# Stick-breaking weights transposed in halves of 64 rows side by side, next to the scores of heads 0 to 3

## The chip, the cores and the metric

The kernel runs on one core of one Trainium2 chip. The metric is the device time of one execution in microseconds (us), taken as the median of several runs. The profile comes from one further execution, recorded by the hardware profiler. Its engines are PE (TensorE matmuls), PEld (TensorE weight loads), DVE (VectorE), ACT (ScalarE), POOL (GpSimd) and SP (SyncE, which issues most of the DMAs).

## What is computed

Two layers over a sequence of 256 positions with 1024 channels, all in float32. Every layer normalizes x, projects it once into all branches, and adds W_out of three gated branches to x: eight heads of dilated attention (branch A), a gated linear recurrence after a short convolution (branch B) and four heads of stick-breaking attention (branch C). The change is in branch C. Cut to it, the reference is:

```python
def hybrid_layer(x, ...):
    hn = rms_norm(x, norm_gain)
    proj = jnp.einsum('bsd,de->bse', hn, w_in)
    a_q, a_k, a_v, a_g, b_x, b_g, c_q, c_k, c_v, c_g = jnp.split(proj, _in_split_points(), axis=-1)
    ...
    y = jnp.concatenate([y_a, y_b, y_c], axis=-1)
    return x + jnp.einsum('bse,ed->bsd', y, w_out)

def stick_breaking_attention(q, k, v):
    ...
        z = jnp.einsum('bhqd,bhkd->bhqk', q_blk, kf) * scale
        causal = key_pos[None, :] < t[:, None]
        log_keep = jnp.where(causal, jax.nn.log_sigmoid(-z), 0.0)
        tail = lax.cumsum(log_keep, axis=3, reverse=True)
        between = jnp.concatenate([tail[..., 1:], jnp.zeros_like(tail[..., :1])], axis=-1)
        weights = jnp.where(causal, jnp.exp(jax.nn.log_sigmoid(z) + between), 0.0)
        return jnp.einsum('bhqk,bhkd->bhqd', weights, vf)
```

## The kernel before, in words

Every projection is cut into chunks of 256 output channels (`CH_CQ`, `CH_CK`, `CH_AQ[0]`, `CH_AK[0]`, `CH_BX`, `CH_AQ[1]`, `CH_AK[1]`, `CH_CG`, `CH_BG` and so on, numbered in the order of their use). A chunk's weights come in two DMAs into staging tiles `st`, of which there are five (`WST`). ACT copies each half of a staging tile into `whi` in a rounded format that PE multiplies faster (line 109), DVE takes the remainder into `wlo` (line 110), and PE multiplies with both. A staging tile is free for the next DMA when both have read it, and `whi` and `wlo` have four buffers each. `weights()` and `ask()` say how far ahead of its use a chunk is requested.

`proj_b` multiplies one chunk in two halves, b = 0 and b = 1. A caller can hand it a function `mid`, whose PE work is put between the halves. PE's order is written by hand (`manual_schedule`); on the other engines a scheduler arranges the instructions of the program when the kernel is built, and each engine then runs its list from front to back.

PSUM has four banks of the pool `at` (tag "s"), three of the pool `pp` and one of `yp`. In layer 0 one `pp` bank holds both halves of a chunk. In layer 1 most chunks are `PAIRED`: each half has a `pp` bank of its own, which is emptied by ACT (`low`, line 335) and then by DVE (line 337).

For branch C, `sb_scores` makes the weights of its four heads, `sw[0..3]`, each a tile of 128 partitions and 384 columns, in 3 blocks of 128 columns. The product with the values needs them transposed. `turned` does that for four blocks at a time: four PE transposes of 128x128 fill one "s" bank, and one ACT copy (line 464) of 128x512 brings it into the tile `wv`. For the twelve blocks there are three such groups. The first stands between the two halves of `CH_BX` (as the `mid` of `conv`), the other two stand after its second half. Then comes the first half of `CH_AQ[1]`, then its `mid`, called `second`: it computes the scores of heads 0 to 3 of branch A (`dil_scores(0)`, PE line 497, four "s" banks: first heads 0 and 1, then heads 2 and 3) and their softmax on DVE (line 504) and ACT (line 83). Then the second half of `CH_AQ[1]`, `CH_AK[1]` and `CH_CG` follow. DVE also computes the convolution of branch B in this stretch (lines 544 and 546).

The transposed weights in `wv` are first read by `values` in `third`, in the `mid` of `CH_BG`, some 20 us later.

Of the kernel before, what the change touches and what calls it, by code (L numbers as in the profile page):

```python
# [12 lines left out]
AF = mybir.ActivationFunctionType  # L13
ALU = mybir.AluOpType

P = 128
# [5 lines left out]
HD = 64  # L22
# [26 lines left out]
def trunk_kernel(ctx: ExitStack, tc: tile.TileContext, x, first_x, first, wpack, prm_d, gatew, gains, consts, rope, out):  # L49
    nc = tc.nc  # L50
    act, dve, pe, gps = nc.scalar, nc.vector, nc.tensor, nc.gpsimd
# [6 lines left out]
    pp = ctx.enter_context(tc.tile_pool(name="pp", bufs=3, space=bass.MemoryType.PSUM))  # L58
    at = ctx.enter_context(tc.tile_pool(name="at", bufs=4, space=bass.MemoryType.PSUM))
    yp = ctx.enter_context(tc.tile_pool(name="yp", bufs=1, space=bass.MemoryType.PSUM))  # L60

    def bank(pool, tag):
        return pool.tile([P, 512], F32, name=tag, tag=tag)
# [6 lines left out]
    def dep(inst, on):  # L70
        tc.add_manual_dep(inst.ins, on.ins.name, nosync)
        return inst
# [3 lines left out]
    def table(name, behind=()):  # L76
        load = act.preload_act_table_set(name)  # L77
        for u in (*loaded["users"], *behind):
            dep(load, u)
        loaded["load"], loaded["users"] = load, []  # L80
# [6 lines left out]
    def v2(a, n=2):  # L87
        return a.rearrange("p (b t) -> p b t", b=n)
# [91 lines left out]
    ident = con[:, C_ID:C_ID + P]  # L180
# [116 lines left out]
    for l in range(L):  # L297
# [50 lines left out]
        def proj_to(dst, c, mid=None, sc=1.0):  # L348
            if l > 0 and c in PAIRED[l]:
                proj_b(c, mid, dst, sc)  # L350
            else:
                scaled(dst, proj_b(c, mid), sc)
# [80 lines left out]
        zs, sw = {}, {}  # L433
        halves = ((0, slice(0, 128)), (1, slice(128, 384)))

        def sb_scores():
# [9 lines left out]
            for h in range(NHC):  # L446
# [8 lines left out]
                                           diag[:, 255 - n:255][:, ::-1], 0.0, ALU.mult, ALU.add)  # L455
                dve.tensor_mul(w, bt, w)

        def turned(tiles, h0, gs, to):
            for g in gs:
                tp = bank(at, "s")  # L460
                for i in range(4):
                    h, j = divmod(4 * g + i, 3)
                    pe.transpose(tp[:, i * P:(i + 1) * P], tiles[h0 + h][:, j * P:(j + 1) * P], ident)  # L463
                act.activation(to[g], tp, AF.Copy)

        def turned_tile():
            wv = wk.tile([P, 1536], F32, name="wv", tag="wv", bufs=1)
            return [wv[:, i:i + 512] for i in range(0, 1536, 512)], by_head(wv[:, 0:1024], wv[:, 1024:1536])

        def by_head(a, b):  # L470
            first = [a[:, 0:384], a[:, 384:768], None, b[:, 128:512]]
            parts = [h if h is None else (h[:, 0:256], h[:, 256:384]) for h in first]
            parts[2] = a[:, 768:1024], b[:, 0:128]
            return parts
# [14 lines left out]
        def dil_scores(h0):  # L489
            sps = {}  # L490
            for p in (h0, h0 + 2):
                for h in (p, p + 1):
                    sps[h] = bank(at, "s")
                for t, cs in halves:
                    for h in (p, p + 1):
                        hr, hb, _ = head(h - h0)
                        pe.matmul(sps[h][:, cs], qT[h0][hr, hb, t * P:(t + 1) * P], kT[h0][hr, hb, 0:(t + 1) * P],  # L497
                                  start=True, stop=True)
            shifted = {}
            for h in range(h0, h0 + 4):  # L500
                xs = scr(384)
                mn = wk.tile([P, 2], F32, name="mn", tag="mn", bufs=4)
                for t, cs in halves:
                    dve.tensor_tensor_reduce(xs[:, cs], sps[h][:, cs], nmask[:, cs], -0.125, 3e38,  # L504
                                             ALU.add, ALU.min, mn[:, t:t + 1])
                shifted[h] = xs, mn
            return shifted

        def dil_softmax(shifted):
            for h, (xs, mn) in shifted.items():  # L510
                pr = wk.tile([P, 384], F32, name="pr", tag="pr", bufs=4)
                den = wk.tile([P, 2], F32, name="den", tag="den", bufs=4)
                for t, cs in halves:
                    tab(pr[:, cs], xs[:, cs], AF.Exp, bias=mn[:, t:t + 1], scale=-1.0, accum_out=den[:, t:t + 1])
                dve.reciprocal(den, den)
                for t, cs in halves:
                    dve.tensor_scalar(pr[:, cs], pr[:, cs], den[:, t:t + 1], None, ALU.mult)
                prob[h] = pr

        def dil_transposes(h0):  # L520
            if h0 == 0:
                a = sb.tile([P, 1024], F32, name="pa", tag="yh1")
                b = sb.tile([P, 512], F32, name="pb", tag="yl1")
                to, heads = (a[:, 0:512], a[:, 512:1024], b), by_head(a, b)
            else:
                to, heads = turned_tile()
            turned(prob, h0, range(3), to)
            return heads

# [10 lines left out]
        def conv(mid):  # L540
            dve.memset(bxp[:, :, 0:3], 0.0)
            proj_to(bxp[:, :, 3:259], CH_BX, mid)
            for b in range(2):
                dve.tensor_scalar(xc[:, b, :], bxp[:, b, 3:259], prm[:, b, 3:4], prm[:, b, 4:5], ALU.mult, ALU.add)
                for j in (2, 1, 0):
                    dve.scalar_tensor_tensor(xc[:, b, :], bxp[:, b, j:j + 256], prm[:, b, j:j + 1], xc[:, b, :],
                                             ALU.mult, ALU.add)
            for j in range(2):
                gps.dma_start(out=xs[j * HD:(j + 1) * HD], in_=xc[(1 - j) * HD:(2 - j) * HD])
# [47 lines left out]
        rotate(proj_b(CH_AQ[0], sb_scores), qT, 0, "q0")  # L597
        rotate(proj_b(CH_AK[0]), kT, 0, "k0")
        sw_t, sw_heads = turned_tile()
        conv(lambda: turned(sw, 0, (0,), sw_t))  # L600
        turned(sw, 0, (1, 2), sw_t)
        y_c = {}

        def second():
            table(LN_EXP)
            dil_softmax(dil_scores(0))

        rotate(proj_b(CH_AQ[1], second), qT, 4, "q1")
        rotate(proj_b(CH_AK[1]), kT, 4, "k1")
        table(SIGM)  # L610
        cg_ps = proj_b(CH_CG)
        pts = dil_transposes(0)
        silu(cg, cg_ps)

# [27 lines left out]
        for n2 in range(2):  # L642
            w = weights(l, CH_O + n2)
            for t in range(NT):
                o_ps[t, n2] = bank(at, "s") if (t, n2) == (0, 0) else bank(pp, "pp")
                out_mm(o_ps[t, n2], w, t, 0, range(4), True, False)
                if (t, n2) == (0, 0):
                    y_c["p"] = dil_transposes(4)
                if (t, n2) == (0, 1):
                    emit_y(values(va, y_c["p"], 4), ag[:, 2:4, :], 6, 2)  # L650
# [125 lines left out]
```

## Time and profile before

| | us |
|---|---|
| median of 3 runs | 249.78 (249.46 to 250.14) |
| the profiled execution's own time | 248.82 |
| its span, first to last instruction | 246.7 |
| PE busy (matmuls) | 239.0 |
| DVE busy | 196.5 |
| ACT busy | 167.2 |
| POOL busy | 12.1 |
| mean granted TensorE clock | 0.996 |

The profiled execution's time is 2.1 us over its span, which is work around the program's own instructions, and 0.96 us under the median of the runs. An instruction row gives the start in us from the start of the span, the length, the engine, the line of the kernel, what it writes and reads, and the number of instructions merged in the row; in brackets stands the idle time before it and what ended it. A row of the chain of waits gives start, length and the work on the path that ended last. A busy PE row is modelled at its end, since matmuls overlap; differences between starts are the safer numbers.

### The profile page before, as it was taken

Reading aid. Unit: us, or ns where it says so; the run is one execution under the profiler, and the core shown is the slowest. Engines: PE = TensorE matmul, PEld = TensorE weight load, DVE = VectorE, ACT = ScalarE, POOL = GpSimd, SP = SyncE. Lnnn points to the kernel's source line nnn. Section 1 sums busy time; section 2 is a strip of 40 time slices with the busy share of each in tenths; the row PEclk is TensorE's granted clock in tenths of the full one; section 3 lists DMA queues with packets and bytes.
Section 4 is the critical chain, followed back from the end, with each engine's and each line's share of the span. In section 5 each row is a group of like instructions: output and inputs, shape, how many; then the busy total and the mean of one; then the engine's idle time right before and its main releaser. Section 6 shows DMA issues by size and latency. Waiting matters only on the chain.

```text
span 246.7 us, 4531 instructions
## 1 busy us (share of the span) xinstructions
PE 239.0 (97%) x1657; PEld 212.1 (86%) x1657; DVE 196.5 (80%) x442; ACT 167.2 (68%) x360; POOL 12.1 (5%) x45
## 2 busy tenths in 40 slices
PE   8999999999999999999999999999999999999990
PEld 4889999999998899878889988889889889987870
DVE  3885699999999799985792766999999987985253
ACT  3778989735947499964662885865498649992142
POOL 0037000001000000000100000000010000000000
PEclk9999999999999999999999999999999999999998
DMA  6989889268447741277157486605553672000022
GB/s 201 404 292 403 342 288 333 96 215 268 134 157 255 258 117 56 85 240 284 74 189 232 142 268 243 200 7 165 161 157 119 197 262 98 0 0 3 0 85 85
DMA packets 13173, 43.89 MB, mean 178 GB/s; under 512 B 1632, under 2 KB 2144, under 8 KB 13152
## 3 DMA queue, kind: packets, MB, share of 16 engines
q1 hardware_dynamic: 12384, 42.30, 51.1%
q10 hardware_dynamic: 576, 0.79, 0.9%
q0 software_dynamic: 192, 0.52, 0.7%
q8 instruction: 13, 0.21, 0.4%
q14 instruction: 8, 0.07, 0.1%
HBM read 42.03 MB, written 1.05 MB: 175 GB/s over the span
## 4 chain that ended last, share of the span: by engine, by line
PE 94%; DMA 2%; DVE 1%; ACT 1%; SPq 0%; issue 0%; ACTq 0%
PE pp L211 51%; PE pp L332 11%; PE s L211 9%; PE pp L329 5%; PE s L169 4%; PE s L463 3%; PE s L497 2%; PE y L427 2%; DMA st<-first 2%; PE pp L169 2%; PE s L443 1%; PE pp L427 1%; PE s L557 1%; PE s L259 1%; DVE xres L668 0%; ACT scr L242 0%
## 5 line engine op out<-in xcount | busy, mean ns | idle before, releaser
L110 DVE TENSOR_TENSOR wlo<-st,whi 128x512 fp32r<-128x512 f32 x132 | 84.1, 683 | 12.8 <-ACT whi L109 12.5
L109 ACT ACTIVATE whi<-st 128x512 fp32r<-128x512 f32 x132 | 73.9, 629 | 28.0 <-PE pp L211 11.8
L211 PE MATMUL pp<-xx,whi 128*128 128x256 f32 x480 | 63.3, 285 | 0.0
L211 PEld LDWEIGHTS pp<-xx,whi 128*128 128x128 f32 x480 | 59.7, 191 | 1.4 <-issue 1.3
L211 PE MATMUL pp<-xx,wlo 128*128 128x256 f32 x240 | 33.7, 283 | 0.0
L211 PEld LDWEIGHTS pp<-xx,wlo 128*128 128x128 f32 x240 | 30.9, 192 | 0.0
L332 PE MATMUL pp<-xx,whi 128*128 128x512 f32 x112 | 29.3, 396 | 0.0
L332 PEld LDWEIGHTS pp<-xx,whi 128*128 128x128 f32 x112 | 20.1, 189 | 4.1 <-ACT scr L83 0.3
L77 ACT ACT_TABLE_LOAD x13 | 16.7, 1283 | 1.9 <-PEq L769 1.7
L83 ACT ACTIVATE pr<-scr,mn 128x128 f32<-128x128 f32 (+1 forms) x32 | 14.1, 442 | 5.2 <-DVE mn L504 5.2
L329 PEld LDWEIGHTS pp<-xx,wlo 128*128 128x128 f32 x112 | 15.3, 190 | 1.1
L329 PE MATMUL pp<-xx,wlo 128*128 128x256 f32 x112 | 15.6, 282 | 0.0
L211 PE MATMUL pp<-whi,yh 128*128 128x512 f32 x48 | 14.5, 403 | 0.0
L211 PE MATMUL pp<-wlo,yh 128*128 128x512 f32 x48 | 14.0, 393 | 0.0
L211 PE MATMUL pp<-whi,yl 128*128 128x512 f32 x48 | 14.0, 393 | 0.0
L335 ACT ACTIVATE low<-pp 128x256 f32<-128x256 f32 x14 | 5.3, 382 | 9.1 <-PE pp L332 6.8
L211 PEld LDWEIGHTS pp<-wlo,yh 128*128 128x128 f32 x48 | 9.0, 188 | 2.1
L211 PEld LDWEIGHTS pp<-whi,yl 128*128 128x128 f32 x48 | 9.0, 188 | 2.0
L211 PEld LDWEIGHTS pp<-whi,yh 128*128 128x128 f32 x48 | 8.6, 188 | 2.0 <-issue 0.3
L169 PE MATMUL s<-whi,xx 128*128 128x512 f32 (+1 forms) x36 | 10.2, 404 | 0.1
L415 ACT ACTIVATE yh<-scr 128x512 fp32r<-128x512 f32 x8 | 5.0, 631 | 7.7 <-DVE scr L413 7.6
L504 DVE CUSTOM_DVE_ANT_0 scr<-s,con 128x128 f32<-128x128 f32 (+1 forms) x32 | 9.2, 351 | 0.0
(165 smaller groups left out, 355.2 us busy)
## 6 DMA issues: line engine op xcount, KB each, us to landing
st<-w_pack SPq DMA_DIRECT2D x66, 512.0 KB, 5.4
st<-first SPq DMA_DIRECT2D x7, 512.0 KB, 6.2
xres<-x_in SPq DMA_DIRECT2D x2, 512.0 KB, 8.1
gw_t<-gate_w SPq DMA_DIRECT2D x2, 256.0 KB, 6.9
gn<-gains SPq DMA_DIRECT2D x1, 512.0 KB, 6.7
xs<-xc POOLq DMA_DIRECT2D x4, 128.0 KB, 3.7
gf<-gains SPq DMA_DIRECT2D x1, 512.0 KB, 6.8
out<-scr SPq DMA_DIRECT2D x2, 256.0 KB, 2.1
```

The costliest lines, as they stand in the source:

```text
L77: load = act.preload_act_table_set(name)
L83: i = dep(act.activation(*a, **k), loaded["load"])
L109: split[l, c] = act.activation(hi[:, ws], st[:, ss], AF.Copy)
L110: dve.tensor_sub(lo[:, ws], st[:, ss], hi[:, ws].bitcast(F32))
L169: pe.matmul(ps[t][:, c0 - base:c1 - base], a[:, k, t * P:(t + 1) * P], b[:, c0:c1], start=k == 0 and i == 0 and c0 == base, stop=k == NK - ...
L211: pe.matmul(ps, a(k), b(k), start=first and i == 0, stop=last and i == len(seq) - 1)
L329: pe.matmul(ps[:, 0:S], lo[:, k, cs], xh[:, k, :], start=False, stop=False, skip_group_check=True)
L332: pe.matmul(ps, hi[:, k, cs], xx[:, k].rearrange("p h t -> p (h t)"), start=i == 0, stop=i == len(seq) - 1, skip_group_check=True)
L335: act.activation(low, ps[:, S:2 * S], AF.Copy, scale=sc)
L427: pe.matmul(y[hr, p * 128 + o:p * 128 + 256], vt[:, s0, hs], wts[i][s0], start=s0 == 0, stop=s0 == 1)
L463: pe.transpose(tp[:, i * P:(i + 1) * P], tiles[h0 + h][:, j * P:(j + 1) * P], ident)
L504: dve.tensor_tensor_reduce(xs[:, cs], sps[h][:, cs], nmask[:, cs], -0.125, 3e38, ALU.add, ALU.min, mn[:, t:t + 1])
```

## The change

The four weight tiles are transposed by a new function `turned_rows`. It takes each block of 128x128 as two halves of 64 rows (r = 0 and r = 64). Each half is a PE transpose of its own, with 64 rows of the block as the stationary operand and a 64x64 piece of the identity as the moving one, and it writes 64 columns of the output. The two halves of a block go to two different PSUM banks, and in the program they follow each other, so that rows 0 to 63 and rows 64 to 127 of the array are used in turn. Blocks 0 to 7 fill two "s" banks; blocks 8 to 11 fill half of each of two `pp` banks. ACT then empties the four banks with four copies (line 467 of the changed kernel), two of 8 runs of 64 columns and two of 4 runs, into the interleaved places of `wv`.

The place changes too. Nothing stands between or behind the halves of `CH_BX` any more. All 24 transposes stand at the beginning of `second`, directly ahead of the scores of heads 0 to 3. Since `CH_BX` has no `mid` now, its `weights()` call requests one chunk more at its start instead of after its first half.

```diff
+        def turned_rows(tiles, to):
+            for b0, b1, pool, tag in ((0, 8, at, "s"), (8, 12, pp, "pp")):
+                tps = [bank(pool, tag) for _ in range(2)]
+                for b in range(b0, b1):
+                    h, j = divmod(b, 3)
+                    for tp, r in zip(tps, (0, HD)):
+                        pe.transpose(tp[:, (b - b0) * HD:(b - b0 + 1) * HD],
+                                     tiles[h][r:r + HD, j * P:(j + 1) * P], ident[r:r + HD, r:r + HD])
+                for tp, r in zip(tps, (0, HD)):
+                    act.activation(to[:, b0:b1, r:r + HD], v2(tp[:, 0:(b1 - b0) * HD], b1 - b0), AF.Copy)
...
-        conv(lambda: turned(sw, 0, (0,), sw_t))
-        turned(sw, 0, (1, 2), sw_t)
+        conv(None)
         y_c = {}
 
         def second():
+            turned_rows(sw, v2(sw_t, 12))
             table(LN_EXP)
             dil_softmax(dil_scores(0))
```

How this moves instructions is seen on three engines. The first place is ACT's list in layer 0, from the table load after the sigmoids of branch C to the first exponential of the softmax; `whi<-st` is the splitting of weights, `wv<-s` the copy out of a transpose bank.

```order
 L77 ACT_TABLE_LOAD
-L109 ACTIVATE whi<-st 128x512 x4
-L464 ACTIVATE wv<-s 128x512
-L109 ACTIVATE whi<-st 128x512 x2
-L464 ACTIVATE wv<-s 128x512 x2
-L109 ACTIVATE whi<-st 128x512 x2
+L109 ACTIVATE whi<-st 128x512 x8
+L467 ACTIVATE wv<-s 128x8x64 x2
+L467 ACTIVATE wv<-pp 128x4x64 x2
 L83 ACTIVATE pr,den<-scr,mn 128x128
```

The same eight splits stand there. Before, the copies stood among them and two splits were left behind the last copy; now all four copies stand behind all eight splits.

The second place is PE's list in layer 1, with buffer numbers and with what each row waits for. Before, from the scores of heads 2 and 3 (`s_2221`, `s_2222`) over the second half of `CH_AQ[1]` (`pp_2285`) to the first half of `CH_AK[1]` (`pp_2326`):

```order
L497 MATMUL s_2221<-k0_2103,q0_2042 128x128 [waits Activation_49]
L497 MATMUL s_2222<-k0_2103,q0_2042 128x128 [waits Activation_49]
L497 MATMUL s_2221<-k0_2103,q0_2042 128x256
L497 MATMUL s_2222<-k0_2103,q0_2042 128x256
L332 MATMUL pp_2285<-xx_1583,whi_2048 128x512 x7
L329 MATMUL pp_2285<-xx_1583,wlo_2049 128x256 x8
L332 MATMUL pp_2285<-xx_1583,whi_2048 128x512
L332 MATMUL pp_2326<-xx_1583,whi_2137 128x512 [waits DVE_49]
```

The same stretch now, where the second half of `CH_AQ[1]` is `pp_2313` and the first half of `CH_AK[1]` is `pp_2354`:

```order
L508 MATMUL s_2249<-k0_2117,q0_2056 128x128 [waits Activation_49]
L508 MATMUL s_2250<-k0_2117,q0_2056 128x128 [waits Activation_49]
L508 MATMUL s_2249<-k0_2117,q0_2056 128x256
L508 MATMUL s_2250<-k0_2117,q0_2056 128x256
L332 MATMUL pp_2313<-xx_1597,whi_2062 128x512 [waits DVE_49]
L332 MATMUL pp_2313<-xx_1597,whi_2062 128x512 x6
L329 MATMUL pp_2313<-xx_1597,wlo_2063 128x256 x8
L332 MATMUL pp_2313<-xx_1597,whi_2062 128x512
L332 MATMUL pp_2354<-xx_1597,whi_2125 128x512 [waits Activation_49]
```

The scores of heads 2 and 3 wait for ACT in both, but now for the copies of the two "s" banks that were filled directly ahead. The second half of `CH_AQ[1]` waits for DVE now: of the three `pp` banks two hold transposes, so it takes the bank of its own first half, which DVE has to empty. The first half of `CH_AK[1]` takes a bank that ACT empties.

The third place is DVE's list in layer 1, from the emptying of the second half of `CH_BX` (`bxp<-pp,low`) to that of the first half of `CH_AQ[1]` (`scr<-pp,low`); `xc` is the convolution, `wlo<-st,whi` the splitting of weights. Before:

```order
L337 TENSOR_TENSOR bxp<-pp,low 128x256
L546 SCALAR_TENSOR_TENSOR xc<-bxp,prm_t,xc 128x256
L544 TENSOR_SCALAR xc<-bxp,prm_t 128x256
L110 TENSOR_TENSOR wlo<-st,whi 128x512
L546 SCALAR_TENSOR_TENSOR xc<-bxp,prm_t,xc 128x256
L110 TENSOR_TENSOR wlo<-st,whi 128x512
L546 SCALAR_TENSOR_TENSOR xc<-bxp,prm_t,xc 128x256
L110 TENSOR_TENSOR wlo<-st,whi 128x512
L546 SCALAR_TENSOR_TENSOR xc<-bxp,prm_t,xc 128x256
L337 TENSOR_TENSOR scr<-pp,low 128x256
```

Now:

```order
L337 TENSOR_TENSOR bxp<-pp,low 128x256
L558 SCALAR_TENSOR_TENSOR xc<-bxp,prm_t,xc 128x256
L556 TENSOR_SCALAR xc<-bxp,prm_t 128x256
L558 SCALAR_TENSOR_TENSOR xc<-bxp,prm_t,xc 128x256 x2
L110 TENSOR_TENSOR wlo<-st,whi 128x512
L558 SCALAR_TENSOR_TENSOR xc<-bxp,prm_t,xc 128x256
L337 TENSOR_TENSOR scr<-pp,low 128x256
```

Between the two rows stand two splits fewer than before, and the first of them has moved ahead of one step of the convolution; that step and the two splits now follow behind the last row.

More of the change, by code (lines that the diff above doesn't have):

```diff
@@ L467, in turned_tile @@
             wv = wk.tile([P, 1536], F32, name="wv", tag="wv", bufs=1)
-            return [wv[:, i:i + 512] for i in range(0, 1536, 512)], by_head(wv[:, 0:1024], wv[:, 1024:1536])
+            return wv, by_head(wv[:, 0:1024], wv[:, 1024:1536])
         def by_head(a, b):
@@ L525, in dil_transposes @@
             else:
-                to, heads = turned_tile()
+                wv, heads = turned_tile()
+                to = [wv[:, i:i + 512] for i in range(0, 1536, 512)]
             turned(prob, h0, range(3), to)
```

## The prediction

> **What bounds the kernel now.** I read the page first: the busy times and the chain that ended last.
>
> ```profile
> PE 239.0 (97%) x1657; PEld 212.1 (86%) x1657; DVE 196.5 (80%) x442; ACT 167.2 (68%) x360; POOL 12.1 (5%) x45
> ...
> PE 94%; DMA 2%; DVE 1%; ACT 1%; SPq 0%; issue 0%; ACTq 0%
> ```
>
> Then the busy times by window, for the stretch between PE's first projection matmul and its last, and for the stretch around the change in layer 1 (columns: the window, then for PE, PEld and DVE the busy us and instructions).
>
> ```profile
> 8.20:240.30 232.10, 232.10 (x1628) 207.44 (x1628) 190.21 (x424) 162.55 (x350) 11.69 (x36) 1.00 0.53 178
> 168.33:176.76 8.43, 8.43 (x61) 7.12 (x59) 8.43 (x20) 4.80 (x10) 0.00 (x0) 1.00 0.58 185
> ```
>
> PE is busy in 232.10 of 232.10 us. So the kernel is PE's list, run without a gap. Two things follow. PE work that is saved counts in full, and so does any wait that PE gets, since nothing later absorbs it. In layer 1 DVE too is busy in 8.43 of 8.43 us: whoever waits there for DVE waits for its list.
>
> The chain of waits gives the stretch of layer 0 (from the end of the first half of `CH_BX` to the end of the scores of heads 0 to 3) and that of layer 1.
>
> ```profile
> 50.66 0.44 PE s L463 x4
> 51.09 2.88 PE pp L211 x24
> 53.98 0.88 PE s L463 x8
> 54.85 2.86 PE pp L211 x24
> 57.72 1.51 PE s L497 x16
> 59.23 14.59 PE pp L211 x120
> ...
> 75.14 2.87 PE pp L211 x24
> ...
> 168.33 0.44 PE s L463 x4
> 168.77 1.62 PE pp L332 x7
> 170.39 0.95 PE pp L329 x8
> 171.34 0.23 PE pp L332
> 171.57 0.88 PE s L463 x8
> ...
> 175.25 1.51 PE s L497 x16
> 176.76 1.82 PE pp L332 x7
> ```
>
> Twelve transposes cost 0.44 + 0.88 = 1.32 us per layer, 0.11 each. A half of a chunk costs 2.87 us in layer 0 and 1.62 + 0.95 + 0.23 = 2.80 in layer 1. The scores next to them cost 1.51. The row at 75.14 is the first half of `CH_BG`.
>
> **The transposes themselves.** The trace has no transpose of 64 rows. The nearest row is the scores (L497), which also run 64 rows at a time in two halves of the array.
>
> ```profile
> L463 PE MATMUL s<-con,sw 128*128 128x128 f32 x24 | 3.3, 272 | 0.0
> L497 PE MATMUL s<-k,q 64*128 64x256 f32 x32 | 4.8, 377 | 0.0
> L497 PE MATMUL s<-k,q 64*128 64x128 f32 x32 | 3.5, 297 | 0.0
> ```
>
> One group of scores is 16 issues, half of them of 256 columns and half of 128. If they run in pairs and time goes with columns, 1.51 us is 4 pairs of one length and 4 of twice that, so a pair of 128 columns takes at most 1.51 / 12 = 0.126 us, and a pair of 64 columns 0.063. Twelve pairs then cost 0.76 us. Other ends: each pair at the price of a whole transpose today, 12 x 0.11 = 1.32; no pairing at all, 24 x 0.11 = 2.64. I take 0.76, since the scores are the nearest row. That saves 0.56 us per layer, if nothing waits.
>
> **The copies in layer 0.** What waits is the second half of the scores. Heads 2 and 3 take the two "s" banks that the transposes have just filled, so ACT must copy both out first. In ACT's list these copies now stand behind all eight splits. Here is ACT around that place, before.
>
> ```profile
> 53.34 1.15 ACT L109 ACTIVATE whi<-st 128x512 fp32r<-128x512 f32 x2 [3.91 <-DMA st<-w_pack]
> 54.40 0.58 ACT L464 ACTIVATE wv<-s 128x512 f32<-128x512 f32 x1
> 54.88 1.16 ACT L109 ACTIVATE whi<-st 128x512 fp32r<-128x512 f32 x2
> 55.94 1.06 ACT L464 ACTIVATE wv<-s 128x512 f32<-128x512 f32 x2
> 58.04 1.15 ACT L109 ACTIVATE whi<-st 128x512 fp32r<-128x512 f32 x2 [1.04 <-DMA st<-w_pack]
> ```
>
> The last pair of splits starts at 58.04, after 1.04 us of waiting for its DMA. It belongs to the second half of `CH_BG`, which PE needs only at 75.14. Before, the copies were done by 57.0, ahead of it. Now they stand behind it. That this transfer does not come earlier is read from the queue's own waits and from the staging tile's landings, of six transfers between 48 and 60 us and of sixteen between 30 and 75:
>
> ```profile
> SPq L106 <- DVE wlo L110: 147.3, 54, 10.8
> ...
> DMA to landing us min/median/max: 4.5/5.1/5.8
> ...
> DMA to landing us min/median/max: 3.6/5.2/6.4
> ```
>
> The issues wait for DVE to free a staging tile, and DVE's list up to there is unchanged. The shortest of the six, 4.5 us, puts the issue at about 53.5 (58.04 - 4.5), and a slower landing makes the splits later.
>
> So in layer 0: the halves of `CH_BX` and `CH_AQ[1]` follow each other without transposes between, 50.66 + 2.88 + 2.86 = 56.40. Transposes to 57.16, the scores of heads 0 and 1 (half of 1.51) to 57.92. ACT begins the first copy about 0.1 before the splits end, as its rows overlap (54.88 + 1.16 against 55.94): 59.09. Two copies, 1.06, end at 60.15. With 0.1 for the hand-over (an estimate, over the 0.03 and 0.04 that ACT's rows of layer 1 below take behind PE) PE goes on at 60.25 and ends the scores at 61.00, against 59.23. **Layer 0: +1.77 us**, with a wait of PE of about 2.3. Behind the waiting matmul stands all of PE's work, since its list is in order. The saving of 0.56 is inside that wait: at 1.32 for the transposes the result is the same, and at 2.64 too (56.40 + 2.64 + 0.76 = 59.80, still before 60.25).
>
> Were ACT free at that moment, the copies alone would set the pace: blocks 0 to 7 are there at 56.40 + 8 x 0.063 = 56.91, two copies end at 58.0, heads 2 and 3 run from 58.1 to 58.86, a gain of 0.37. The loss above comes from the late turn of the copies and not from their length.
>
> [...]
>
> **The bank in layer 1.** ACT keeps up with PE here. Its rows before: a copy directly behind the transposes (PE's row ends at 168.33 + 0.44 = 168.77), `low` of the first half of `CH_AQ[1]` directly behind that half (it ends at 175.25), and an idle stretch ahead of the softmax.
>
> ```profile
> 168.80 0.60 ACT L464 ACTIVATE wv<-s 128x512 f32<-128x512 f32 x1
> ...
> 175.29 0.38 ACT L335 ACTIVATE low<-pp 128x256 f32<-128x256 f32 x1 [0.24 <-PE pp L332]
> 179.12 0.40 ACT L83 ACTIVATE pr<-scr,mn 128x128 f32<-128x128 f32 x1 [3.45 <-DVE mn L504]
> ```
>
> The second half of `CH_AQ[1]`, though, needs the bank of its first half, and DVE empties that. DVE's rows before:
>
> ```profile
> 173.41 0.68 DVE L110 TENSOR_TENSOR wlo<-st,whi 128x512 fp32r<-128x512 f32 x1
> 174.02 0.48 DVE L546 SCALAR_TENSOR_TENSOR xc<-bxp,prm_t,xc 128x256 f32<-128x256 f32 x1
> 174.41 0.42 DVE L337 TENSOR_TENSOR bxp<-pp,low 128x256 f32<-128x256 f32 x1
> 174.75 0.48 DVE L546 SCALAR_TENSOR_TENSOR xc<-bxp,prm_t,xc 128x256 f32<-128x256 f32 x1
> 175.14 0.41 DVE L544 TENSOR_SCALAR xc<-bxp,prm_t 128x256 f32<-128x256 f32 x1
> 175.47 0.69 DVE L110 TENSOR_TENSOR wlo<-st,whi 128x512 fp32r<-128x512 f32 x1
> 176.07 0.48 DVE L546 SCALAR_TENSOR_TENSOR xc<-bxp,prm_t,xc 128x256 f32<-128x256 f32 x1
> ...
> 178.46 0.41 DVE L337 TENSOR_TENSOR scr<-pp,low 128x256 f32<-128x256 f32 x1
> ```
>
> From start to start a split takes 0.60, L546 0.39, L337 0.34, L544 0.33. In the new order, from 173.41: split to 174.02, `bxp` (L337) to 174.36, then L546 174.75, L544 175.08, two L546 175.86, split 176.46, L546 176.85, and L337 ends 0.42 later, at 177.27. With 0.1 for the hand-over PE goes on at 177.37.
>
> PE gets there at 168.33 + 2.80 + 2.80 = 173.93, transposes to 174.69, heads 0 and 1 to 175.45. The copies: `low` of `CH_AQ[1]` is done at 173.93 + 0.04 + 0.38 = 174.35, the last of blocks 0 to 7 at 173.93 + 0.51 = 174.44; two copies end at 175.53, and heads 2 and 3 run from 175.63 to 176.39. Then the wait for DVE, 0.98 us, to 177.37, against 176.76. **Layer 1: +0.61 us.** Unpaired transposes (2.64) would put the end of the scores at 173.93 + 2.64 + 1.51 = 178.08, +1.32. If that bank were free, it would be 176.39, -0.37.
>
> The rest I put at nothing: ACT has one copy more (0.3 us by half of L464's 0.58), in a place where it then waits for the softmax; the earlier request for weights leaves SP's order of transfers as it was; the first read of `wv` is 20 us away. PE resumes in a full stream behind each wait, and DVE, ACT and the DMAs then lead it by more than before.
>
> **Sum:** 1.77 + 0.61 = +2.38 us. Against the profiled execution's own 248.82 (span 246.7 and 2.1 around it) that is 251.2. The median of the runs is 0.96 above that execution; the prediction is for the median, 249.78 + 2.38 = 252.2.
>
> **The rivals.**
> - *The copies come in time: faster.* If the transfer for `CH_BG` were there 2.4 us earlier, or the copies got their turn ahead of the splits, and the bank were free, both layers would gain 0.37: 249.0. With no copy in the way at all it would be 2 x 0.56 = 1.12: 248.7. It decides at 57.92: the second copy must be done by then, so the splits by about 56.9 and the landing by 55.7, 2.2 us after the issue. The shortest of the landings above, 4.5, speaks against it, and so does ACT's order. Chance 0.08.
> - *No change.* Waits as in the first rival, but each pair takes the 0.11 of today's transpose. Then the copies start 0.35 later in each layer and the two gains shrink to about nothing: 249.8. Chance 0.08. [...]
> - *Only layer 0 waits.* The bank is free in time: +1.77 - 0.37 = 1.40, 251.2. For it speaks that DVE's list could run a little earlier behind the wait of layer 0; against it that DVE is full in the stretch. Chance 0.14.
> - *The change doesn't do what it says.* The halves run one after the other: 1.77 + 1.32 = 3.09, 252.9. Against it speaks that 16 score issues fit in 1.51 us. Chance 0.15.
> - My forecast, both waits with paired halves: 0.55.
>
> **How the numbers follow.** 0.3% is 0.75 us, about what a measurement of this kernel can tell from no change. Three cases end above it, 0.55 + 0.14 + 0.15 = 0.84 for slower, 0.08 each for the same and faster. For the range: with only layer 0 waiting and its transfer landing after 3.6 us, the shortest of the sixteen, instead of 4.5, it is 249.78 + 1.40 - 0.9 = 250.3; with the slowest of the six, 5.8, my forecast becomes 249.78 + 2.38 + 1.3 = 253.5. So 250.3 to 253.5, which leaves out the first two rivals, 0.16.
>
> **What would show it.** In the profile after: PE with a gap of 2 us or so at about 58 us, ended by ACT's copy (L467), and ACT's copies directly behind a split that waited for its DMA; a second gap of 0.5 to 1 us in layer 1 at the second half of `CH_AQ[1]`, ended by DVE's L337; the 24 transposes in 0.7 to 0.8 us. I am wrong if PE has no gap there, if the copies start before 58 us, or if the transposes take over 1.4.

## The result, and the profile after

The changed kernel takes 251.88 us (median of 6 runs, 251.44 to 256.57), the kernel before 249.88 (6 runs): ratio 1.0079, 95% interval 1.0061 to 1.0097, slower by about 2.0 us (0.79% of 249.88). Forecast were 252.2 and a range of 250.3 to 253.5. The run of 256.57 us, at a mean granted clock of 0.978, is left out of the ratio; there is no trace of it.

The profiled execution took 252.11 us with a span of 250.1. The busy times and the chain that ended last, now:

```profile
PE 239.2 (96%) x1681; PEld 211.0 (84%) x1681; DVE 196.5 (79%) x442; ACT 167.5 (67%) x362; POOL 11.4 (5%) x45
...
PE 77%; DVE 12%; DMA 4%; ACT 4%; issue 2%; SPq 0%; DVEq 0%; ACTq 0%
```

The busy times have hardly moved; the chain has. Before, it was PE for 94%; now a sixth of it runs over DVE and ACT, so PE's list is no longer without gaps. In layer 0 it leaves PE at 39.82 and runs over DVE's list, up to the split that frees the staging tile for one transfer (L110, 54.34 to 54.96). How it gets back to PE from there is in the chain itself (start, length, what):

```profile
54.98 3.91 DMA st<-w_pack
58.88 0.02 issue
58.91 1.15 ACT whi L109 x2
60.06 0.49 ACT wv L467
60.55 0.04 issue
60.59 0.48 PE s L508 x2
61.08 0.00 issue
61.08 0.92 PE s L508 x4
62.00 4.01 PE pp L211 x32
```

Read from the top: a transfer of weights, the two splits that wait for it, the first copy of the transposes, and only then PE's scores of heads 2 and 3. The timeline of the same place, PE and ACT, says how long PE stood:

```profile
57.82 0.71 PE L464 MATMUL s<-con,sw 64*128 64x64 f32 x16
58.37 0.41 PE L464 MATMUL pp<-con,sw 64*128 64x64 f32 x8
58.62 0.88 PE L508 MATMUL s<-k,q 64*128 64x128 f32 x8
60.59 1.41 PE L508 MATMUL s<-k,q 64*128 64x128 f32 x8 [1.10 <-ACT wv L467]
...
58.91 1.15 ACT L109 ACTIVATE whi<-st 128x512 fp32r<-128x512 f32 x2 [1.59 <-DMA st<-w_pack]
59.96 1.06 ACT L467 ACTIVATE wv<-s 128x512 f32<-128x512 f32 x2
```

The 24 transposes start at 57.82 and the scores behind them at 58.62: 0.80 us, where the twelve whole ones took 1.32, so the pairs do overlap. PE then idles for 1.10 us until the first copy is done, and the rows behind 60.59 stretch to 1.41 because head 3 waits once more, for the second copy (it ends at 59.96 + 1.06 = 61.02; PE's next step in the chain starts at 61.08).

Layer 1, PE and DVE:

```profile
176.57 0.71 PE L464 MATMUL s<-con,sw 64*128 64x64 f32 x16
177.12 0.56 PE L464 MATMUL pp<-con,sw 64*128 64x64 f32 x8
177.47 1.91 PE L508 MATMUL s<-k,q 64*128 64x128 f32 x16
179.59 0.41 DVE L337 TENSOR_TENSOR scr<-pp,low 128x256 f32<-128x256 f32 x1
180.06 1.89 PE L332 MATMUL pp<-xx,whi 128*128 128x512 f32 x7 [0.69 <-DVE scr L337]
```

The second gap, 0.69 us, ends with DVE's L337, as forecast, at the second half of `CH_AQ[1]`.

To compare kernels I take one stretch per layer out of each chain or timeline: from the start of the stick-breaking scores (L443) to the end of the scores of heads 0 to 3. Before it is 37.43 to 59.23 and 155.44 to 176.76, now 38.91 to 62.00 and 158.18 to 180.06. So layer 0 goes from 21.80 to 23.09, **+1.29**, and layer 1 from 21.32 to 21.88, **+0.56**: +1.85 together, which the measured 2.0 (0.0061 to 0.0097 of 249.88 is 1.5 to 2.4) holds. The spans differ by more, 3.4 us, but most of the rest stands ahead of the change: the stretch of layer 0 already begins 1.48 later. The first loads of weights, before and after:

```profile
1.64 4.93 DMA st<-first
```

```profile
1.65 6.08 DMA st<-first
```

They took 1.15 us longer in this execution. The kernels below start their stretch anywhere between 37.9 and 38.9 us, and the medians average over that.

### The profile page after: what moved, and what is told of

The parts are those of the page before. It is cut to its first block, busy times and chain, and to the rows that moved or that the text cites. A ratio compares the mean times of both kernels' runs of the same rounds, so it can differ in the third digit from the quotient of the medians.

```text
span 250.1 us, 4578 instructions
## 1 busy us (share of the span) xinstructions
PE 239.2 (96%) x1681; PEld 211.0 (84%) x1681; DVE 196.5 (79%) x442; ACT 167.5 (67%) x362; POOL 11.4 (5%) x45
## 4 chain that ended last, share of the span: by engine, by line
PE 77%; DVE 12%; DMA 4%; ACT 4%; issue 2%; SPq 0%; DVEq 0%; ACTq 0%
PE pp L211 44%; PE s L211 9%; PE pp L332 6%; PE s L169 4%; PE pp L329 3%; DVE wlo L110 3%; DMA st<-first 2%; PE y L427 2%; PE s L474 2%; PE pp L169 2%; PE s L508 2%; DMA st<-w_pack 2%; DVE sw L454 1%; ACT scr L83 1%; DVE scr L492 1%
## 5 line engine op out<-in xcount | busy, mean ns | idle before, releaser
L110 DVE TENSOR_TENSOR wlo<-st,whi 128x512 fp32r<-128x512 f32 x132 | 84.0, 683 | 12.5 <-ACT whi L109 12.3
L211 PE MATMUL pp<-xx,whi 128*128 128x256 f32 x480 | 63.6, 285 | 0.0
L211 PEld LDWEIGHTS pp<-xx,whi 128*128 128x128 f32 x480 | 59.8, 191 | 1.7 <-issue 1.3
L211 PE MATMUL pp<-xx,wlo 128*128 128x256 f32 x240 | 33.7, 283 | 0.0
L211 PEld LDWEIGHTS pp<-xx,wlo 128*128 128x128 f32 x240 | 30.9, 192 | 0.0
L211 PE MATMUL pp<-whi,yh 128*128 128x512 f32 x48 | 14.5, 404 | 0.0
L211 PE MATMUL pp<-wlo,yh 128*128 128x512 f32 x48 | 14.0, 393 | 0.0
L211 PE MATMUL pp<-whi,yl 128*128 128x512 f32 x48 | 14.0, 393 | 0.0
L169 PE MATMUL s<-whi,xx 128*128 128x512 f32 (+1 forms) x36 | 9.5, 379 | 1.5 <-ACT xx L153 1.4
L211 PEld LDWEIGHTS pp<-wlo,yh 128*128 128x128 f32 x48 | 9.0, 188 | 2.1
L211 PEld LDWEIGHTS pp<-whi,yl 128*128 128x128 f32 x48 | 9.0, 188 | 2.0
L211 PEld LDWEIGHTS pp<-whi,yh 128*128 128x128 f32 x48 | 8.6, 188 | 2.0 <-issue 0.3
```

The source lines that it names most:

```text
L110: dve.tensor_sub(lo[:, ws], st[:, ss], hi[:, ws].bitcast(F32))
L169: pe.matmul(ps[t][:, c0 - base:c1 - base], a[:, k, t * P:(t + 1) * P], b[:, c0:c1], start=k == 0 and i == 0 and c0 == base, stop=k == NK - ...
L211: pe.matmul(ps, a(k), b(k), start=first and i == 0, stop=last and i == len(seq) - 1)
```

## The experiments

The theory is the forecast's: the place costs two waits of PE, for ACT's late copies in layer 0 and for a bank in layer 1, and the halves themselves save 0.56 us per layer. The rival is that the transposing by halves is what costs. All ratios are to the kernel before, of runs on the same chip. `dep(a, b)` in the diffs keeps instruction a behind b on its engine.

**Only the move.** Whole transposes in the new place (they fill three "s" banks, and no `pp` bank):

```
-            turned_rows(sw, v2(sw_t, 12))
+            turned(sw, 0, range(3), [sw_t[:, i:i + 512] for i in range(0, 1536, 512)])
```

> Only the move: the transposes stand next to the scores of heads 0 to 3 as in the changed kernel, but whole, 128 by 128, in three banks of the scores' pool, with three copies of ACT. Theory (the waits cost the time, the halves cost nothing by themselves): in layer 0 PE still waits for ACT, whose copies stand behind the splits that wait for the transfer of CH_BG; the splits end at about 59.9 us on the changed kernel's clock, three copies of 0.53 end at about 61.5, so the scores end at 62.3 or so, +1.6 us against before; in layer 1 no bank of the projections is taken, so the wait for DVE's L337 is gone and the stretch is within 0.2 of before. Sum +1.6: 251.5 us, ratio 1.006. Rival (what costs is the transposing by halves, the switching of the array or the interleaved copies, and the place costs nothing): the time of before, 249.9 us, ratio 1.000.

Measured: 253.66 us (251.85 to 254.6), ratio 1.0143 (1.011 to 1.0175). The rival is out: there is not a single half-transpose in this kernel, and it is slower than the whole change. It isn't the place alone, though: with three of the four "s" banks taken, heads 1 to 3 wait for copies and not only heads 2 and 3, so 2 of the 16 issues of the scores run ahead of the wait and not 8. Layer 1 came out as expected (160.65 to 182.15 is 21.50, +0.18). But the time is 2 us above the theory's. Part of that, in the traced run, is the transfer, 5.13 us long where it took 3.91 in the changed kernel; for the rest the theory had nothing. Here are the transfer (from the chain) and the wait (from the timeline), then the granted clock (in a row of the windows it is the third number from the end), then the block of projections behind the scores:

```profile
54.24 5.13 DMA st<-w_pack
```

```profile
61.08 2.62 PE L508 MATMUL s<-k,q 64*128 64x128 f32 x14 [2.17 <-ACT wv L475]
```

```profile
60.00:62.00 2.00, 0.92 (x8) 0.78 (x8) 1.62 (x5) 2.00 (x5) 0.84 (x2) 0.99 0.51 207
62.00:64.00 2.00, 2.00 (x8) 1.29 (x8) 1.70 (x13) 1.85 (x10) 0.41 (x1) 0.50 0.66 141
64.00:66.00 2.00, 2.00 (x13) 2.00 (x13) 2.00 (x11) 1.98 (x10) 0.00 (x0) 0.65 0.77 252
66.00:68.00 2.00, 2.00 (x19) 2.00 (x19) 2.00 (x10) 1.99 (x3) 0.00 (x0) 1.00 0.09 12
```

```profile
63.70 15.35 PE pp L211 x120
```

PE stood for 2.17 us, and right behind that its granted clock is 0.50 and then 0.65 for some 4 us. The 120 matmuls behind, 14.59 us before, take 15.35, and the scores are stretched too (14 issues in 2.62 us). Of the six runs the four with a mean clock of 0.988 or 0.989 took 253.56 to 254.6, the two at 0.995 and 0.997 took 251.85 and 252.28, which is near the theory's 251.5. So a second cost was suspected: that this gap also costs clock. Why two of the six runs do not show it stays open.

**The gap filled with work.** The same kernel, with twelve idle transposes in layer 0 (four blocks done four times into the same place; the output is unchanged):

```
-                for i in range(4):
+                for i in list(range(4)) * (4 if tiles is sw and l == 0 and g == 2 else 1):
```

> The kernel with only the move (whole transposes next to the scores), with twelve transposes more in layer 0: the four of the third bank are done four times over (the same numbers into the same place), 1.31 us of work without use, in PE's wait. Theory (the granted clock fell to 0.5 and 0.65 for 4 us behind the gap of 2.2 us of PE there, and that cost 1.9 us on top of the wait itself): the gap is 0.9 us now, the clock stays at 1.00, and with more work the kernel is faster: 251.7 us, ratio 1.008, against 253.7 and 1.014. Rival (the granted clock there fell by chance, or for another reason than the gap): 253.7 us as before. Second rival (the added work lengthens the path): 255.0.

Measured: 252.18 us (251.85 to 252.7, five runs), ratio 1.0095 (1.0079 to 1.0111): with 1.31 us more of PE work (24 transposes from 57.11 to 59.83, with only the move twelve from 57.01 to 58.42), 1.5 us faster than only the move (by the ratios 0.0048 x 249.7 = 1.2, though the two intervals just touch). The second rival, 255.0, is out. Against the first, chance, speaks that the clock was low in four of six runs there and in none of five here; it is not shut out. One more thing is not the same: three splits stand ahead of the softmax in DVE's list, at 61 us, and not behind it. No run here tells that apart from the filling. PE's wait and the clock there:

```profile
57.11 2.79 PE L474 MATMUL s<-con,sw 128*128 128x128 f32 x24
59.83 0.49 PE L508 MATMUL s<-k,q 64*128 64x128 f32 x2
61.01 1.89 PE L508 MATMUL s<-k,q 64*128 64x128 f32 x14 [0.69 <-ACT wv L475]
```

```profile
62.00:64.00 2.00, 2.00 (x16) 1.67 (x16) 2.00 (x8) 0.39 (x2) 0.67 (x3) 1.00 0.59 139
64.00:66.00 2.00, 2.00 (x19) 2.00 (x18) 2.00 (x15) 2.00 (x11) 0.00 (x0) 1.00 0.99 330
```

The scores go on at the same moment (61.01 against 61.08), so the filled time was free, and the clock stays at 1.00; all five runs lie at mean clocks of 0.993 to 0.997. The same 14 issues take 1.89 us here and 2.62 with only the move, and the block of 120 matmuls behind them 14.58 and 15.35: 0.73 + 0.77 = 1.5 us, which is the difference of the two traced executions (254.22 and 252.70).

So the clock fell behind a gap of 2.17 us, in the traced run and, by the mean clocks, in three more of six. With 2.79 us of transposes where 1.48 stood, and 0.69 us of waiting left, it stayed at 1.00 in the one trace.

**Only the halves.** The 24 half transposes behind `CH_BX` and ahead of `CH_AQ[1]`, with all four banks from the scores' pool:

```
-            for b0, b1, pool, tag in ((0, 8, at, "s"), (8, 12, pp, "pp")):
+            for b0, b1, pool, tag in ((0, 8, at, "s"), (8, 12, at, "s")):
...
+        turned_rows(sw, v2(sw_t, 12))
         def second():
-            turned_rows(sw, v2(sw_t, 12))
```

> Only the halves: the same 24 transposes of 64 rows, but directly behind CH_BX, ahead of the first half of CH_AQ[1], with all four banks from the scores' pool. Theory: the 2.8 us of CH_AQ[1] behind them cover the four copies, so PE waits for nothing; the 24 transposes cost 0.75 us for 1.32 before, less what entering and leaving the halves costs (0.1 to 0.2 per layer): 0.4 to 0.55 gained in each layer, 248.8 to 249.2 us, ratio 0.996 to 0.998. Rival (the halves cost it, wherever they stand): 251 us or more, ratio 1.005 to 1.008.

Measured: 249.52 us (249.07 to 249.85), ratio 0.9987 (0.9977 to 0.9997). The halves don't cost, against the rival; but they save less than expected, 0.3 us in all. Its chain in layer 0:

```profile
54.73 0.89 PE s L464 x24
55.62 3.06 PE pp L211 x24
58.68 1.51 PE s L508 x16
```

Here is where the rest went: the transposes take 0.89, and the half of `CH_AQ[1]` behind them 3.06 instead of the 2.86 that it took behind whole transposes. Together 0.89 + 0.20 = 1.09 against 1.32 before, 0.23 saved in layer 0 (the two stretches are 0.24 and 0.25 shorter). Going from whole rows to halves and back costs PE's stream 0.13 ahead (0.89 less twelve pairs of 0.063) and 0.20 behind, and in this place it is paid for the transposes and again for the scores.

**Copies first.** The changed kernel, the late split behind the copies in layer 0:

```
-                split[l, c] = act.activation(hi[:, ws], st[:, ss], AF.Copy)
+                split[l, c] = act.activation(hi[:, ws], st[:, ss], AF.Copy); (l, c, i) == (0, CH_BG, 1) and dep(split[l, c], copied[-1])
```

> The changed kernel, with ACT's order alone altered in layer 0: the split of the second half of CH_BG stands behind the four copies, not ahead of them. Theory (the copies' late turn behind a split that waits for its transfer is the cost of layer 0): PE's wait there of 1.5 to 2 us goes, the stretch of layer 0 ends 0.3 to 0.45 earlier than before the change, layer 1 keeps its +0.56: about 250.1 us, ratio 1.001. Rival (the wait is not the cost of layer 0, or the copies themselves are too long): the changed kernel's time, 251.9 us, ratio 1.008.

Measured: 250.3 us (249.94 to 250.43), ratio 1.0017 (1.0006 to 1.0029). The time of layer 0's wait is gone, as expected, though the layer is only 0.09 below before and not 0.3 to 0.45. ACT, and PE's chain:

```profile
58.23 1.09 ACT L467 ACTIVATE wv<-s 128x512 f32<-128x512 f32 x2 [1.39 <-PE pp L464]
59.20 0.67 ACT L467 ACTIVATE wv<-pp 128x256 f32<-128x256 f32 x2
59.73 1.17 ACT L109 ACTIVATE whi<-st 128x512 fp32r<-128x512 f32 x2
```

```profile
57.56 0.64 PE s L464 x16
58.20 0.25 PE pp L464 x8
58.45 1.84 PE s L508 x14
60.29 14.59 PE pp L211 x120
```

The copies now start at 58.23, just behind the first eight blocks (58.20), and the splits stand behind them. From the first transpose to the last score it is 2.73 us (57.56 to 60.29), against 1.32 + 1.51 = 2.83 before. Layer 1 keeps its +0.57 (156.48 to 178.37).

**A free bank.** The changed kernel, with the attention output's bank in place of the second projection bank:

```
-            for b0, b1, pool, tag in ((0, 8, at, "s"), (8, 12, pp, "pp")):
-                tps = [bank(pool, tag) for _ in range(2)]
+            for b0, b1, banks in ((0, 8, ((at, "s"), (at, "s"))), (8, 12, ((pp, "pp"), (yp, "y")))):
+                tps = [bank(*p) for p in banks]
```

> The changed kernel, with one of the two projection banks of the last four blocks taken from the attention output's pool, so that the second half of CH_AQ[1] no longer needs the bank that DVE's L337 empties. Theory (that bank is the cost of layer 1): the wait of 0.7 us there goes, the stretch of layer 1 ends 0.2 to 0.4 earlier than before the change, layer 0 stays as it is: 251.0 us, ratio 1.004. Rival (DVE's list is the limit there whatever bank it is, and the wait comes back behind): the changed kernel's time, 251.9 us, ratio 1.008.

Measured: 251.75 us (250.77 to 253.91), ratio 1.0092 (1.0058 to 1.0127). By the time alone this tells nothing: the six runs scatter by more than the 0.9 us in question. One of them, at 253.08, has a low mean clock (0.986), as with only the move; the slowest, at 253.91, has 0.990, hardly less than the traced run's 0.991, so its time is not explained. The trace tells it, though:

```profile
177.55 1.84 PE s L508 x14
179.39 1.81 PE pp L332 x7
```

The projection follows the scores without a wait; the stretch is 158.19 to 179.39, 21.20, 0.68 shorter than in the changed kernel. Layer 0 was 23.65 in this execution, +1.85 against before, since its transfer took longer:

```profile
54.41 4.48 DMA st<-w_pack
```

That is 4.48 us, against 3.91 in the changed kernel: 0.57 more, and the layer is 0.56 longer.

**Both.** The last two diffs together:

> Both cures in the changed kernel: the split of CH_BG's second half behind the four copies in layer 0, and one of the last two banks from the attention output's pool. Theory (the two waits are all of the loss, and they are independent): the stretch of layer 0 as in the kernel with copies first (-0.09 against before), that of layer 1 as in the kernel with the free bank (-0.12): 249.5 us, ratio 0.999, 0.8 us below copies first alone. Rival (one wait's time comes back somewhere else once the other is gone): 250.3 us or more, ratio 1.002 and up.

Measured: 249.54 us (249.19 to 250.45), ratio 0.9988 (0.9976 to 1.0001), by the ratios 0.7 us below copies first. The stretches are 38.01 to 59.72 and 155.92 to 177.12, -0.09 and -0.12, the very figures of the two kernels with one cure each. So the two waits were all of the loss, and they are independent.

**Small group first.** The copies-first diff, and the order and banks of the two groups changed:

```
-            for b0, b1, pool, tag in ((0, 8, at, "s"), (8, 12, pp, "pp")):
-                tps = [bank(pool, tag) for _ in range(2)]
+            for b0, b1, banks in ((8, 12, ((at, "s"), (at, "s"))), (0, 8, ((pp, "pp"), (yp, "y")))):
+                tps = [bank(*p) for p in banks]
```

> The place and the halves of the change without any wait: the four last blocks are transposed first, into two of the scores' banks, then the first eight into one projection bank and the attention output's bank; in layer 0 the split of CH_BG's second half stands behind the copies. Heads 2 and 3 then need only the two short copies (0.33 us each), which end while PE still transposes the eight blocks and runs heads 0 and 1. Theory (what was left of the loss with copies first, 0.4 us per layer, is PE's wait for the two long copies): PE runs through, transposes 0.9 us with the entry into the halves and scores 1.4, so each layer gains 0.5 against before: 248.7 us, ratio 0.996. Rival (the rest is the cost of the halves themselves, no wait): the time of the kernel with both cures, 249.5, ratio 0.999.

Measured: 248.95 us (248.14 to 249.73), ratio 0.9964 (0.9948 to 0.998), faster than both kernels. ACT's two short copies, PE's chain in layer 0 and the ends of the stretch in layer 1:

```profile
57.30 0.66 ACT L467 ACTIVATE wv<-s 128x256 f32<-128x256 f32 x2 [0.83 <-PE s L464]
```

```profile
56.87 0.39 PE s L464 x8
...
57.76 1.37 PE s L508 x16
59.13 6.89 PE pp L211 x56
```

```profile
155.24 1.58 PE L443 MATMUL s<-kc,qc 64*128 64x128 f32 x16
...
175.96 1.88 PE L332 MATMUL pp<-xx,whi 128*128 128x512 f32 x7
```

PE runs through the stretch of layer 0. Transposes and scores take 59.13 - 56.87 = 2.26 us, 0.57 below before, and the 16 issues of the scores 1.37 instead of 1.51, which fits halves that are entered once, ahead of the transposes (0.13 by the kernel with only the halves). Layer 1 is 20.72, -0.60, but 0.22 of that is lost again further on: up to 184.83 PE waits for DVE's L337, which empties a bank (the weight loads of L211 wait 0.5 us for L337). The measured gain is 0.9 and not 1.16.

All stretches (us, and against before), and the measured difference by the ratio. A trace is of one execution: that of only the move took 254.22 and that of the gap filled 252.70, both some 0.5 above their medians.

| kernel | layer 0 | layer 1 | measured |
|---|---|---|---|
| before | 21.80 | 21.32 | |
| after | 23.09 (+1.29) | 21.88 (+0.56) | +2.0 |
| only the move | 25.51 (+3.71), and 0.76 in the block behind | 21.50 (+0.18) | +3.6 |
| the gap filled | 24.61 (+2.81) | 21.51 (+0.19) | +2.4 |
| only the halves | 21.56 (-0.24) | 21.07 (-0.25) | -0.3 |
| copies first | 21.71 (-0.09) | 21.89 (+0.57) | +0.4 |
| a free bank | 23.65 (+1.85) | 21.20 (-0.12) | +2.3 |
| both | 21.71 (-0.09) | 21.20 (-0.12) | -0.3 |
| small group first | 21.24 (-0.56) | 20.72 (-0.60) | -0.9 |

## Why the prediction was right

- **Layer 0, the wait for ACT.** The mechanism held: PE stops at the scores of heads 2 and 3, the copies stand behind the splits for `CH_BG`, and putting them ahead takes 1.5 us off (by the ratios, 1.0079 to 1.0017). The size was +1.29, not +1.77. On the clock of before (1.48 off) the copies started at 59.96 - 1.48 = 58.48 instead of 59.09, 0.61 earlier, because the transfer took 3.91 us and not the 4.5 that was taken for it. Against that the scores ended 0.98 behind the second copy and not 0.85: head 3 cannot start before it. 1.77 - 0.61 + 0.13 = 1.29. PE's standstill has another form than forecast, 1.10 us and not 2 or more: PE goes on behind the first copy already and stops once more for the second. The transfer takes from 3.91 to 5.13 us in the chains of the four kernels that wait there, and this term goes with it.
- **Layer 1, the bank.** +0.56 for +0.61. DVE's L337 ended at 180.00 - 2.74 = 177.26 on the clock of before (2.74 is what its stretch starts later), where the walk through DVE's list gave 177.27; PE went on at 177.32, where 177.37 was forecast.
- **The transposes.** 0.76 per layer was forecast, 0.063 a pair. From the first pair to the scores it is 0.80 in layer 0 (57.82 to 58.62) and 0.90 in layer 1 (176.57 to 177.47), of which the entry into the halves is part. So the rival with 0.11 a pair is out. One weight load takes about as long with 64 rows as with 128 (the profile's medians are 139 ns for L464 in the kernel after and 141 for L463 before); but 24 of them pass in those 0.80 us, so they overlap.
- **The halves one after the other.** Out for the same reason.
- **Only layer 0 waits.** Out: 0.69 us of PE's wait in layer 1 ended with L337.
- **Copies in time.** Its price, 0.37 per layer, was too high: with both waits cured it is 0.09 and 0.12. The sum there let the copies start 0.51 behind the first transpose and the scores end 0.86 behind the second copy; in the kernel with copies first it is 0.67 (57.56 to 58.23) and 0.97 (58.23 + 1.09 = 59.32 to 60.29). So PE still waits 0.47 (2.73 against 2.26) for two copies of 512 columns. That is a third limit, behind the two waits: with short copies in their place 0.56 and 0.60 are gained, the saving of 0.56 that the transposes promise.
- **What the forecast did not have** is a price of a gap beyond its length. In the changed kernel's trace there is none: the granted clock is 1.00 in each window of two us from 58 to 68. Behind the gap of 2.17 us of the kernel with only the move there is one, 1.5 us in its trace. The forecast's own 2.3 us of wait would have been of that size, so it was luck that the term could be left out. Whether the run of 256.57 us met it stays open.

## What to carry to other kernels

When PE work is moved, look at who has to empty its banks and what already stands in that engine's list at that moment: here the splits that waited 1.59 us for their transfer held up the copies behind them, and a saving of 0.56 us turned into a loss of 1.29. Bring the first-needed small copies ahead, and give the big ones banks that nobody wants soon: the kernel with the small group first does both and stands at -0.9 us, where the changed kernel stands at +2.0. In a kernel in which PE never stops, look at the granted clock behind a gap of some 2 us: in the one trace here that shows it fall, a gap of 2.17 us cost 1.5 us more than its length.

## What the runs showed of the hardware

- A gap of 2.17 us in PE's list (only the move) was followed by a granted clock of 0.50 and 0.65 for 4 us; gaps of 0.69 (the gap filled), 1.10 (the changed kernel) and 1.67 us (a free bank) were not (1.00 in the windows behind them). With twelve useless transposes in the gap, which left the 0.69 us, the clock stayed at 1.00. That the gap is the cause is likely but rests on one trace of each and on the mean clocks of eleven runs.
- A pair of fp32 transposes of 64 rows takes about 0.063 us (with the small group first, eight pairs start between 57.10 and 57.60, the two of a pair within 0.01 us of each other), a whole one 0.11 (only the move, layer 1: twelve in 1.31 us).
- Going from whole rows to the two halves of the array costs about 0.13 us and back 0.20 (only the halves: 0.89 us for twelve pairs, then 3.06 for a half of a chunk that took 2.86), so work by halves is cheaper next to other work by halves: it saves 0.56 and 0.60 us in the two layers beside the scores (small group first), 0.24 and 0.25 away from them (only the halves).
- In the rounded format 24 projection matmuls of 256 columns take 2.88 us (the kernel before, L211 at 51.09), 0.47 ns a column; its twelve whole transposes of 128 columns, in plain fp32, take 1.32 us, 0.86 ns a column. The two rows differ in shape too.
